# First feed-forward with four pairs by seven in seven of its groups, raw weight tiles also in unwritten places of its result, a fourth sum kept apart, another head and other ends

## Chip, core and metric

The kernel runs on one core of one Trainium2 chip. The metric is device time in microseconds (us) of one execution; the median of several runs is compared. A core has five engines that run their own instruction streams: PE (TensorE, matrix products; "PEld" are its weight loads), DVE (VectorE), ACT (ScalarE), POOL (GpSimd) and SP (SyncE, which here only issues DMAs). They wait for one another and for DMAs by semaphores.

## What is computed

One layer on x of 256 tokens by 2048, in float32, with 256 memory tokens. Cut to what matters here:

```python
def swiglu_ffn(h, w_in, w_out):
    gate, up = jnp.split(h @ w_in, 2, axis=-1)
    return (jax.nn.silu(gate) * up) @ w_out

x = x + 0.5 * swiglu_ffn(rms_norm(x, ffn1_norm), ffn1_w_in, ffn1_w_out)
...
x = x + memory_cross_attention(h, mem_n, w_q, w_kv, w_o)
x = x + 0.5 * swiglu_ffn(rms_norm(x, ffn2_norm), ffn2_w_in, ffn2_w_out)
return rms_norm(x, final_norm)
```

w_in is 2048 by 11264 (gate and up columns), w_out 5632 by 2048. The change touches h @ w_in of both feed-forwards (FF1, FF2), the start of the kernel, the end of the w_o product in front of FF2, and the final norm.

## The kernel before

**Split products.** A float32 operand a is held as hi = a rounded to fp32r and lo = a − hi. A product is hi·hi + hi·lo + lo·hi, so three matmuls. ACT makes hi by a cast, DVE lo by a subtraction (`parts`, L339 and L340); the pair of them is an `hl` tile.

**Groups.** A feed-forward's w_in product runs over 11 groups j of 512 gate and 512 up columns, and in a group over 16 row tiles k of 128 rows of w_in, taken in 8 pairs. A row tile of a group is a raw tile of 128x1024 (512 KB), loaded by SP (L349). Token columns are two halves of 128.
- A pair "by eight" (`eight`, through `by_two`: L288 x_hi·w_hi, L289 x_hi·w_lo, L291 x_lo·w_hi) is 2 row tiles with 12 matmuls of 512 columns each: 24.
- A pair "by seven" (`seven`, through `three`: L275, L276, L277) is Strassen's scheme in Winograd's form on a 2 by 2 block of row tiles and halves: seven products, 21 matmuls. It needs sums of raw tiles on DVE (L388, L389, L394, L401), which are split like weights, and sums of x (the "forms", made by `sides`, L368 to L376: two operations of ACT, four of DVE, a split).

A pattern of letters says which pair goes how: both feed-forwards have "SCSCSCCC" (S by seven, C by eight) in groups 1 to 10, 183 matmuls each; group 0 is plain, by eight throughout, 192. The results of the products 1 to 7 and of the eighth accumulator stay in eight PSUM banks through a group; behind the last S, ACT and DVE add them up (L439 to L443, L452), and `give` (L418, L420) makes silu(gate)·up into h[j].

**Accumulated weights.** For the row tiles in `SUMMED` (2, 7, 13 of each group but the first) the low part is made by a DMA: `summed` has ACT write −raw, rounded, into the low part (L358) and raw, rounded, into the high part (L359), and POOL issue a DMA that adds the weight onto the low part, so that raw − hi stands there (L360). It costs ACT one more pass and DVE none. FF1 has two such tiles (`hl_s`, and one in `more`, which takes x's place after group 0), FF2 one.

**Places.** Raw tiles cycle over four tiles of a pool and five places in `spare`; hl tiles over three of a pool, two in `ring`, in FF1 two more in `more`. In FF2, `spare` lies in the place that the attention's o_hl has before (tag S2), `ring` in S0.

**Head.** For k = 0 to 15 of FF1's group 0: SP loads two tiles of x (`x_arrives`), ACT and DVE make gain·x as hi and lo (`gained`, L239, L240), the weight is loaded, split and multiplied; `x_more` loads x once more by rows in four chunks of 512 KB at k = 5, 7, 9, 11, into raw tiles, and ACT squares them (L525) for the norm; at k = 6, 9, 12 the forms are made.

**Order.** A tile scheduler sets the order of each engine from the program's order and its own estimates; `issue_after` ties an instruction behind another. Engines take their instructions in order: a waiting one holds up all behind it. Per group SP issues 16 loads, ACT's and POOL's accumulations lie between the casts.

## Time and profile before

| | before |
|---|---|
| median of 3 runs | 2108.14 us (2107.7 to 2108.7) |
| profiled execution: its time | 2108.84 us |
| profiled execution: span from the first to the last instruction | 2107.0 us |
| PE busy | 2084.5 us (99%) |
| DVE busy | 1576.8 us (75%) |
| ACT busy | 1161.6 us (55%) |
| mean granted TensorE clock | 0.998 |

Rows of the timeline read: start, duration (both us), engine, line of the kernel, operation, output<-inputs, shape, count, and in brackets how long the engine had been idle before it and what released it. Matmuls overlap: a row's duration is longer than the distance to the next start. Rows of the waits read: what waited, for what, us in total, times, longest. Times in texts below are us from the span's start.

### The profile page before, as it was taken

To read this page: it belongs to the slowest core of one execution; us is meant where nothing else is said; L and a number is where in the kernel's file an instruction comes from. 1 tells how busy PE (TensorE), PEld (TensorE's weight loads), DVE (VectorE), ACT (ScalarE), POOL (GpSimd) and SP (SyncE) were. 2 spreads that over 40 slices of the span, in tenths; PEclk is the share of its full clock that TensorE was granted. 3 is DMA by queue.
4 is the path that set the end of the run, shared out by engine and by line. 5 is a ranking of instruction groups with operands and counts; after the bars stand their busy time and mean duration, and the time that the engine had idled before them with its cause. 6 is when DMAs were issued, how large, how long until landed. Compare 5 with 4: busy or idle time off the path is not lost.

```text
span 2107.0 us, 26590 instructions
## 1 busy us (share of the span) xinstructions
PE 2084.5 (99%) x9764; PEld 1738.5 (83%) x9764; DVE 1576.8 (75%) x2215; ACT 1161.6 (55%) x1450; POOL 67.7 (3%) x83
## 2 busy tenths in 40 slices
...
GB/s 360 230 227 257 229 238 245 263 167 169 216 198 188 206 236 200 190 176 185 176 201 185 186 154 111 206 281 191 231 259 247 232 229 250 178 160 202 197 192 149
DMA packets 122244, 442.34 MB, mean 210 GB/s; under 512 B 13697, under 2 KB 13825, under 8 KB 121729
## 3 DMA queue, kind: packets, MB, share of 16 engines
...
q10 hardware_dynamic: 288, 0.79, 0.1%
q14 instruction: 56, 0.45, 0.1%
...
## 4 chain that ended last, share of the span: by engine, by line
PE 84%; issue 11%; DMA 2%; ACT 1%; POOL 1%; DVE 1%; SPq 0%; POOLq 0%; ACTq 0%
PE acc L172 12%; PE acc L173 12%; PE acc L171 12%; PE acc L125 9%; PE acc L289 7%; PE acc L288 7%; PE acc L291 7%; PE acc L126 4%; PE acc L277 2%; PE acc L276 2%; PE acc L275 2%; PE aux L263 1%; PE acc L1066 1%; PE acc L1065 1%; PE acc L1067 1%
## 5 line engine op out<-in xcount | busy, mean ns | idle before, releaser
L113 DVE TENSOR_TENSOR hl<-raw,hl 128x1024 fp32r<-128x1024 f32 (+1 forms) x402 | 488.6, 1216 | 282.5 <-ACT hl L112 281.1
L112 ACT CAST hl<-raw 128x1024 fp32r<-128x1024 f32 (+1 forms) x402 | 419.7, 1045 | 481.6 <-PE acc L173 289.3
L339 ACT CAST hl<-spare 128x1024 fp32r<-128x1024 f32 (+1 forms) x135 | 131.8, 993 | 95.5 <-DVE spare L389 38.5
L340 DVE TENSOR_TENSOR hl<-spare,hl 128x1024 fp32r<-128x1024 f32 (+1 forms) x135 | 154.4, 1150 | 35.8 <-ACT hl L339 34.2
L288 PE MATMUL acc<-hl,x_hl 128*128 128x512 f32 x408 | 144.2, 394 | 9.7 <-ACT hl L339 9.7
L289 PE MATMUL acc<-hl,x_hl 128*128 128x512 f32 x408 | 149.9, 395 | 0.0
L340 DVE TENSOR_TENSOR hl<-raw,hl 128x1024 fp32r<-128x1024 f32 (+1 forms) x101 | 113.9, 1131 | 45.9 <-ACT hl L339 44.3
L339 ACT CAST ring<-spare 128x1024 fp32r<-128x1024 f32 (+1 forms) x99 | 97.2, 988 | 68.9 <-DVE spare L389 26.9
L340 DVE TENSOR_TENSOR ring<-spare,ring 128x1024 fp32r<-128x1024 f32 (+1 forms) x99 | 112.9, 1145 | 19.9 <-ACT ring L339 18.8
L291 PE MATMUL acc<-hl,x_hl 128*128 128x512 f32 x408 | 127.5, 392 | 0.0
L339 ACT CAST hl<-raw 128x1024 fp32r<-128x1024 f32 (+1 forms) x101 | 97.7, 977 | 51.8 <-PE acc L291 16.1
L172 PE MATMUL acc<-hl,x_hl 128*128 128x512 f32 x256 | 100.5, 392 | 0.2 <-DVE hl L113 0.2
L172 PE MATMUL acc<-hl,m_hl 128*128 128x512 f32 x256 | 100.4, 392 | 0.0
L173 PE MATMUL acc<-hl,m_hl 128*128 128x512 f32 x256 | 100.2, 391 | 0.0
L173 PE MATMUL acc<-hl,x_hl 128*128 128x512 f32 x256 | 99.8, 390 | 0.0
L288 PEld LDWEIGHTS acc<-hl,x_hl 128*128 128x128 f32 x408 | 76.8, 189 | 25.9 <-ACT hl L339 10.1
L289 PE MATMUL acc<-ring,x_hl 128*128 128x512 f32 x248 | 93.1, 389 | 0.0
L288 PE MATMUL acc<-ring,x_hl 128*128 128x512 f32 x248 | 91.2, 390 | 0.0
L171 PE MATMUL acc<-hl,m_hl 128*128 128x512 f32 x256 | 91.2, 393 | 0.0
L289 PEld LDWEIGHTS acc<-hl,x_hl 128*128 128x128 f32 x408 | 77.2, 190 | 16.9 <-DVE hl L340 1.1
L291 PEld LDWEIGHTS acc<-hl,x_hl 128*128 128x128 f32 x408 | 77.5, 190 | 16.4
L125 PE MATMUL acc<-x_hl,hl 128*128 128x512 f32 x256 | 91.0, 398 | 0.0
(359 smaller groups left out, 5173.9 us busy)
## 6 DMA issues: line engine op xcount, KB each, us to landing
spare<-in_ffn_w_in SPq DMA_DIRECT2D x192, 512.0 KB, 6.4
raw<-in_ffn_w_out SPq DMA_DIRECT2D x176, 512.0 KB, 3.8
raw<-in_ffn_w_in SPq DMA_DIRECT2D x160, 512.0 KB, 6.3
hl_s<-in_ffn_w_in POOLq DMA_DIRECT2D x44, 512.0 KB, 7.3
raw<-in_w_mix_vg SPq DMA_DIRECT2D x32, 512.0 KB, 4.6
raw<-in_w_k SPq DMA_DIRECT2D x32, 512.0 KB, 4.0
raw<-in_w_v SPq DMA_DIRECT2D x32, 512.0 KB, 4.4
raw<-in_w_mix_out SPq DMA_DIRECT2D x32, 512.0 KB, 4.6
```

Source lines behind the costliest of these rows:

```text
L112: nc.scalar.copy(out=hl[:, 0, :size], in_=raw[:, :size])
L113: newest[0] = nc.vector.tensor_tensor(out=hl[:, 1, :size], in0=raw[:, :size], in1=hl[:, 0, :size].bitcast(F32), op=ALU.subtract)
L125: nc.tensor.matmul(acc, lhsT=w_hi, rhs=x_hl, start=first, stop=False, skip_group_check=True)
L126: nc.tensor.matmul(acc[:, 0], lhsT=w_lo, rhs=x_hl[:, 0], start=False, stop=last, skip_group_check=True)
L171: nc.tensor.matmul(acc[t], lhsT=x[:, 0, s], rhs=hi[:, k], start=k0 + k == 0, stop=False)
L172: nc.tensor.matmul(acc[t], lhsT=x[:, 0, s], rhs=lo[:, k], start=False, stop=False)
L173: nc.tensor.matmul(acc[t], lhsT=x[:, 1, s], rhs=hi[:, k], start=False, stop=k0 + k == nk - 1)
L288: nc.tensor.matmul(acc[t][g], lhsT=x[:, 0, s], rhs=hi[:, cols[g]], start=(t, g) in first, stop=False)
L289: nc.tensor.matmul(acc[t][g], lhsT=x[:, 0, s], rhs=lo[:, cols[g]], start=False, stop=False)
L291: nc.tensor.matmul(acc[t][g], lhsT=x[:, 1, s], rhs=hi[:, cols[g]], start=False, stop=last)
L339: nc.scalar.copy(out=hl[:, 0, :n], in_=raw[:, :n])
L340: newest[0] = nc.vector.tensor_tensor(out=hl[:, 1, :n], in0=raw[:, :n], in1=hl[:, 0, :n].bitcast(F32), op=ALU.subtract)
```

## The change

- FF1: groups 1 to 7 go by "SCSCSCSC" (four pairs by seven), with the row tiles 2, 6, 7, 11 and 14 accumulated; groups 8 to 10 as before. Its raw tiles also cycle over h[j] tiles that aren't written yet (`h[max(j + 2, 7):]`); accumulated weights have raw places of their own, and `summed` for the next one is issued one row tile later.
- `seven`: the sum for product 4 is written into the free half of `sums`, ahead of the splits, no longer into `two`.
- FF2: group 0 goes by "SCSCSCCC" too, 183 matmuls instead of 192. Its forms are made beside the w_o product, behind x's tiles 1, 5 and 9, with a raw tile as scratch; `ring` is allocated there.
- Head: 11 matmuls of 128 columns on a tile of ones, whose result isn't used; x's first tile and FF1's gains come in one DMA on ACT's queue; the first weight in two halves, each split by itself; x's chunks for the squares at k = 2, 4, 6, 8 into h[7] to h[4]; forms at k = 6, 9, 12, 15.
- End: three of the four sums of squares are added up ahead of the last; the last enters the root and the mean directly; a tensor_scalar takes the place of a scalar_tensor_tensor.

By count of the order, 8460 matmuls of 512 columns become 8430; those of 256 columns stay 964; those of 128 columns become 304 + 11.

```diff
-PATTERNS = ("SCSCSCCC", "SCSCSCCC")
-SUMMED = ((2, 7, 13), (2, 7, 13))
+FOUR, THREE = "SCSCSCSC", "SCSCSCCC"
+SUMMED = {FOUR: (2, 6, 7, 11, 14), THREE: (2, 7, 13)}
+WARM = 11
...
+    gx = xt.tile([P, 2 * KD + KD * T], F32, name="gx", tag="x")
+    gains, xT = gx[:, KD:2 * KD], gx[:, 2 * KD:].rearrange("p (k t) -> p k t", t=T)
+    nc.scalar.dma_start(out=gx[:, KD:2 * KD + T], in_=a["gains_x0"])
+    nc.scalar.dma_start(out=xT[:, 1], in_=a["xT"][:, 1])
+    nc.vector.memset(ones, 1.0)
+    idle = pa.tile([P, 2, T], F32, name="aux")
+    for _ in range(WARM):
+        nc.tensor.matmul(idle[:, 0, :P], lhsT=ones, rhs=ones, start=True, stop=True)
+    nc.scalar.activation(out=st.tile([P, 1], F32, name="warm"), in_=ones[:, 0:1], func=AF.Silu)
...
+    def sides(k, gain, form, xg, f):
+        xg = xg.rearrange("p (k t) -> p k t", k=2)
+        f = f.rearrange("p (f n) -> p f n", f=4)
+        for q in range(2):
+            nc.scalar.activation(out=xg[:, q], in_=xT[:, k + q], func=AF.Copy, scale=gain(k + q))
+        a11, a21, a12, a22 = xg[:, 0, :P], xg[:, 0, P:], xg[:, 1, :P], xg[:, 1, P:]
+        nc.vector.scalar_tensor_tensor(out=f[:, 0], in0=a21, scalar=-1.0, in1=a22, op0=ALU.mult, op1=ALU.subtract)
+        nc.vector.scalar_tensor_tensor(out=f[:, 1], in0=f[:, 0], scalar=-1.0, in1=a11, op0=ALU.mult, op1=ALU.subtract)
+        nc.vector.tensor_tensor(out=f[:, 2], in0=a11, in1=a21, op=ALU.subtract)
+        nc.vector.tensor_tensor(out=f[:, 3], in0=a12, in1=f[:, 1], op=ALU.subtract)
+        split(form[:, :, 0], form[:, :, 1], f)
...
+            self.raws_summed = [self.raws.pop()]
...
+            raws = self.raws + [h.rearrange("p a b -> p (a b)") for h in self.h[max(j + 2, NG - 4):]]
+            i = self.raw_at % (4 + len(raws))
             self.raw_at += 1
-            raw = wraw.tile([P, 1024], F32, name="raw") if i < 4 else self.raws[i - 4]
+            raw = wraw.tile([P, 1024], F32, name="raw") if i < 4 else raws[i - 4]
             nc.sync.dma_start(out=raw, in_=self.w_in[j, :, k])
...
-            raw, hl = self.raw(j, k), self.hls[at % len(self.hls)]
+            raw, hl = self.raws_summed[at % len(self.hls)], self.hls[at % len(self.hls)]
+            nc.sync.dma_start(out=raw, in_=self.w_in[j, :, k])
...
+            nc.vector.tensor_tensor(out=sums[:, lo], in0=two[:, lo], in1=one[:, lo], op=ALU.subtract)
...
-            nc.vector.tensor_tensor(out=two[:, lo], in0=two[:, lo], in1=one[:, lo], op=ALU.subtract)
-            w = self.parts(two, G)
+            w = self.parts(sums, G)
             three(b["4"], self.x(k + 1, 1), w[:, 0, lo], w[:, 1, lo], first, False)
+            if self.next is not None:
+                with tc.issue_after(self.cast.ins):
+                    self.summed(self.next)
+                self.next = None
...
-                if at is not False:
-                    self.summed(at + len(self.hls))
+                if self.next is not None:
+                    with tc.issue_after(self.cast.ins):
+                        self.summed(self.next)
+                self.next = None if at is False else at + len(self.hls)
...
+        def rooted(self, root):
+            r = root()
+            nc.scalar.activation(out=st.tile([P, 1], F32, name="warm"), in_=ones[:, 0:1], func=AF.Silu)
+            self.summed(0)
+            return r
+        def early(self, before):
+            self.raw_at += 1
+            self.at += 1
+            raw = wraw.tile([P, 1024], F32, name="raw")
+            hl = whl.tile([P, 2, 1024], F32R, name="hl")
+            halves = [slice(G, 2 * G), slice(0, G)]
+            for s in halves:
+                nc.sync.dma_start(out=raw[:, s], in_=self.w_in[0, :, 0, s])
+            x = before(0)
+            for s in halves:
+                with tc.issue_after(x.ins):
+                    split(hl[:, 0, s], hl[:, 1, s], raw[:, s])
+            return hl
+        def run(self, root, before=None, after=None, more=None, early=False):
+            self.sums_at = [(j, k) for j in range(1, NG) for k in SUMMED[self.patterns[j]] if j < NG - 1 or k < 13]
+            if early:
+                acc = token_accs()
+                for k in range(KD):
+                    if k == 0:
+                        w = self.early(before)
+                    else:
+                        before(k)
+                        w = self.parts(self.raw(0, k))
+                    begin = [(t, g) for t in range(2) for g in range(2)] if k == 0 else []
+                    by_two(acc, self.x_hl[:, k], w[:, 0], w[:, 1], k, begin, k == KD - 1)
+                    after(k)
+                    if k == 13:
+                        r = self.rooted(root)
+                self.give(0, [acc[t][0] for t in range(2)], [acc[t][1] for t in range(2)], r)
+                if more is not None:
+                    more()
+                    self.summed(1)
+            else:
+                r = self.group(0, None, root=root)
...
-        raw = wraw.tile([P, 1024], F32, name="raw")
+        raw = ff.h[7 - c].rearrange("p a b -> p (a b)")
...
-            if k in (5, 7, 9, 11):
-                x_squares(k // 2 - 2)
-            if k in (6, 9, 12):
+                nc.sync.dma_start(out=pv, in_=a["pv"])
+            if k in (2, 4, 6, 8):
+                x_squares(k // 2 - 1)
+            if k in (6, 9, 12, 15):
...
-        ff = FeedForward(stack, ("S1", "S0", "S2"), x_hl, "ffn1_norm", a["ffn1_w_in"], PATTERNS[0], SUMMED[0])
+        ff = FeedForward(stack, ("S1", "S0", "S2"), x_hl, lambda k: gains[:, k:k + 1], a["ffn1_w_in"], [FOUR] * 8 + [THREE] * (NG - 8))
...
+            ring = big.tile([P, 4, 2, 1024], F32R, name="ring", tag="S0")
+            done = [2 * p + 1 for p, c in enumerate(THREE) if c == "S"]
...
+                if f in done:
+                    raw = wraw.tile([P, 1024], F32, name="raw")
+                    sides(f - 1, lambda k: col("ffn2_norm", k), forms_in(ring)[done.index(f)], raw[:, :512], raw[:, 512:])
...
-        ff = FeedForward(stack, ("S0", "S1", "S2"), x_hl, "ffn2_norm", a["ffn2_w_in"], PATTERNS[1], SUMMED[1])
+        ff = FeedForward(stack, ("S0", "S1", "S2"), x_hl, lambda k: col("ffn2_norm", k), a["ffn2_w_in"], [THREE] * NG, ring)
...
-            tot, v, s, r = [st.tile([P, 1], F32, name=f"{n}{t}") for n in ("f_tot", "f_v", "f_s", "f_r")]
-            nc.vector.reduce_sum(out=tot, in_=sums[:, t], axis=AX.X)
-            nc.scalar.activation(out=s, in_=tot, func=AF.Sqrt, scale=1.0 / D, bias=eps)
-            nc.vector.tensor_scalar(out=v, in0=tot, scalar1=1.0 / D, scalar2=RMS_EPS, op0=ALU.mult, op1=ALU.add)
+            v, s, r = [st.tile([P, 1], F32, name=f"{n}{t}") for n in ("f_v", "f_s", "f_r")]
+            last = sums[:, t, 3:4]
+            nc.scalar.activation(out=s, in_=last, func=AF.Sqrt, scale=1.0 / D, bias=most[t])
+            nc.vector.tensor_scalar(out=v, in0=last, scalar1=1.0 / D, scalar2=most[t], op0=ALU.mult, op1=ALU.add)
             nc.vector.reciprocal(out=r, in_=s)
-            nc.vector.scalar_tensor_tensor(out=r, in0=v, scalar=r, in1=s, op0=ALU.mult, op1=ALU.add)
+            nc.vector.tensor_scalar(out=r, in0=v, scalar1=r, scalar2=s, op0=ALU.mult, op1=ALU.add)
...
+        most = [st.tile([P, 1], F32, name=f"f_most{t}") for t in range(2)]
+        for t in range(2):
+            nc.vector.reduce_sum(out=most[t], in_=sums[:, t, 0:3], axis=AX.X)
+            nc.vector.tensor_scalar(
+                out=most[t], in0=most[t], scalar1=1.0 / D, scalar2=RMS_EPS, op0=ALU.mult, op1=ALU.add
+            )
```

At the start of the program, PE's first rows were those of row tile 0 (`acc` the accumulators, `hl` the split weight, `x_hl` the split x):

```order
L288 MATMUL acc<-hl,x_hl 128x512 x4
L289 MATMUL acc<-hl,x_hl 128x512 x2
L291 MATMUL acc<-hl,x_hl 128x512 x2
L289 MATMUL acc<-hl,x_hl 128x512 x2
L291 MATMUL acc<-hl,x_hl 128x512 x2
L288 MATMUL acc<-hl,x_hl 128x512 x4
```

and are now

```order
L203 MATMUL aux<-ones 128x128 x11
L302 MATMUL acc<-hl,x_hl 128x512
L303 MATMUL acc<-hl,x_hl 128x512
L305 MATMUL acc<-hl,x_hl 128x512
L302 MATMUL acc<-hl,x_hl 128x512 x2
L303 MATMUL acc<-hl,x_hl 128x512
L302 MATMUL acc<-hl,x_hl 128x512
L305 MATMUL acc<-hl,x_hl 128x512
L303 MATMUL acc<-hl,x_hl 128x512
L305 MATMUL acc<-hl,x_hl 128x512
```

The 11 idle matmuls stand first; then the first row tile begins with one accumulator, whose three products come together, since the weight comes by halves.

In FF1's groups ACT makes the accumulated tiles between the casts (`hl_s` and `more` the two tiles that are accumulated onto, `raw` and `spare` raw weights; the brackets name the semaphores waited for, DMASW that of an accumulating DMA). Before, at the turn from group 1 to group 2:

```order
L339 CAST ring_117<-spare_118 128x1024 [waits PE_49,Activation_49]
L339 CAST more_475<-raw_859 128x1024 [waits DMAHW4_49,PE_49,Activation_49]
L418 ACTIVATE h1_107<-spare_118,r_x2_95 128x512 [waits DVE_49]
L339 CAST hl_882<-raw_861 128x1024 [waits DMAHW5_49,PE_49,Activation_49]
L358 ACTIVATE more_475<-raw_838 128x1024 [waits DMAHW0_49,DMASW3_49,PE_49]
L359 CAST more_475<-raw_838 128x1024 [waits PE_49]
L339 CAST hl_892<-raw_861 128x512 [waits DVE_49,Activation_49]
L339 CAST hl_899<-spare_118 128x1024 [waits DMAHW0_49,Activation_49]
L339 CAST ring_117<-spare_118 128x1024 [waits PE_49,Activation_49]
```

Now, in group 5, for its row tiles 11 and 14 (on the tiles that row tiles 6 and 7 leave):

```order
L378 CAST ring_131<-raw_1885 128x1024 [waits DMAHW6_49,PE_49,Activation_49]
L378 CAST hl_1875<-spare_132 128x512 [waits DVE_49]
L399 ACTIVATE more_498<-spare_132 128x1024 [waits DMAHW7_49,DMASW5_49,PE_49]
L400 CAST more_498<-spare_132 128x1024 [waits PE_49]
L399 ACTIVATE hl_s_133<-spare_132 128x1024 [waits DMAHW2_49,DMASW6_49,PE_49]
L378 CAST ring_131<-spare_132 128x1024 [waits DVE_49,Activation_49]
L400 CAST hl_s_133<-spare_132 128x1024 [waits PE_49,Activation_49]
L378 CAST more_498<-raw_1913 128x1024 [waits DVE_49,DMAHW1_49,PE_49,Activation_49]
L378 CAST hl_1937<-raw_1915 128x1024 [waits PE_49,Activation_49]
```

Two accumulations (L399, L400) now stand next to one another, where one stood alone; each waits for the low matmuls that read its tile last, and the casts behind wait with it. On PE there are, in the order, 54, 41, 41, 57, 41, 38 and 34 matmuls of 512 columns between the last low matmul on the tile that row tile 7 uses and the first low matmul of row tile 7, in groups 1 to 7; 48 to 50 for row tile 11; more than 53 for the others. Before, the smallest such distance was 103 in FF1 and 43 in FF2.

At the start of FF2, PE went from w_o's last matmuls (L126) on to plain products of group 0:

```order
L126 MATMUL acc_11040<-o_hl_9109,hl_11064 128x256
L125 MATMUL acc_11040<-o_hl_9109,hl_11064 128x512
L126 MATMUL acc_11040<-o_hl_9109,hl_11064 128x256
L288 MATMUL acc_11114<-hl_11120,x_hl_10402 128x512 [waits Activation_49]
L288 MATMUL acc_11115<-hl_11120,x_hl_10402 128x512 [waits PE_49]
```

and now goes to products of the first pair by seven:

```order
L128 MATMUL acc_11116<-o_hl_9157,hl_11140 128x512
L129 MATMUL acc_11116<-o_hl_9157,hl_11140 128x256
L128 MATMUL acc_11116<-o_hl_9157,hl_11140 128x512
L129 MATMUL acc_11116<-o_hl_9157,hl_11140 128x256
L289 MATMUL acc_11189<-hl_11203,ring_10452 128x512 [waits Activation_49]
L289 MATMUL aux_11190<-hl_11203,ring_10452 128x512
L290 MATMUL acc_11189<-hl_11203,ring_10452 128x512 [waits DVE_49]
```

On DVE, at the same place, `xT` is the residual's last tile, and `spare` the place of the sums. Now:

```order
L379 TENSOR_TENSOR ring_10452<-raw_11237,ring_10452 128x1024 [waits DMAHW4_49,Activation_49]
L253 SCALAR_TENSOR_TENSOR x_hl_10450<-xT_3513,pv_82,x_hl_10450 128x256 [waits Activation_49]
L229 TENSOR_TENSOR ss_10451<-ss_10451,sq_11113 128x256 [waits Activation_49]
L265 SCALAR_TENSOR_TENSOR xT_3513<-acc_11116,xT_3513 128x256 [waits PE_49]
L416 TENSOR_TENSOR spare_11187<-raw_11197 128x512 [waits DMAHW2_49]
L417 TENSOR_TENSOR spare_11187<-raw_11199,raw_11197 128x512 [waits DMAHW3_49]
L265 SCALAR_TENSOR_TENSOR xT_3513<-acc_11116,xT_3513 128x256 [waits DVE_49]
L422 TENSOR_TENSOR raw_11197<-spare_11187,raw_11199 128x512 [waits DVE_49]
L379 TENSOR_TENSOR hl_11203<-spare_11187,hl_11203 128x1024 [waits Activation_49]
```

The weight that PE needs first (hl_11203) is the split of a sum in `spare`; the sums stand behind the residual of w_o's last product (acc_11116), half of which lies between them. Before, the weight needed first was split straight from a raw tile.

112 lines of the change are left out of this document (42 added, 70 removed).

## The prediction

> **What bounds the kernel now.** I read the page's busy shares and its chain first, then TensorE's (PE's) waits, then windows by stage. All times are us.
>
> ```profile
> PE 2084.5 (99%) x9764; PEld 1738.5 (83%) x9764; DVE 1576.8 (75%) x2215; ACT 1161.6 (55%) x1450; POOL 67.7 (3%) x83
> PE 84%; issue 11%; DMA 2%; ACT 1%; POOL 1%; DVE 1%; SPq 0%; POOLq 0%; ACTq 0%
> ```
> ```profile
> PE acc L288 <- ACT hl L339: 9.7, 2, 7.1
> PE acc L289 <- DMA hl_s<-in_ffn_w_in: 1.0, 2, 0.7
> PE acc L275 <- ACT h L418: 0.5, 1, 0.5
> ```
> ```profile
> 10.00:60.00 50.00, 46.95 (x195) 37.44 (x194) 33.32 (x54) 37.22 (x54) 1.88 (x2) 0.97 0.91 340
> 160.00:210.00 50.00, 50.00 (x223) 41.40 (x222) 40.30 (x49) 32.18 (x36) 3.48 (x4) 1.00 0.79 251
> 1320.00:1380.00 60.00, 60.00 (x348) 52.49 (x347) 45.54 (x72) 32.01 (x46) 0.00 (x0) 1.00 0.62 199
> ```
>
> PE is busy 99% and carries the chain. It waits about 12 us in the whole program, 9.7 of them at two places of the head. So two things pay: fewer matmuls, and the head. The windows (columns: PE, weight loads, DVE, ACT, POOL, granted clock, DMA share, GB/s) show the head below clock 1.00 and with PE gaps of 3 in 50; in the feed-forward's steady stage (160 to 210) PE has no gap, DVE is at 81%, ACT 64%, the DMA engines 79%.
>
> **1. Fewer matmuls.** One matmul of 512 columns in the steady stream costs its start-to-start distance:
>
> ```profile
> 17.39 0.39 PE L288 MATMUL acc<-ring,x_hl 128*128 128x512 f32 x1
> ...
> 22.84 0.39 PE L288 MATMUL acc<-hl,x_hl 128*128 128x512 f32 x1
> ```
> Between these rows lie two row tiles k of 12 matmuls: 5.45/24 = 0.227 each, 2.72 per k. A pair by eight has 24, by seven 21. In the order, FF1 has one pair more by seven in groups 1 to 7 (21 matmuls fewer), FF2 three in group 0 (9 fewer): **−4.8 and −2.0**.
>
> **2. Head.**
> ```profile
> 6.01 1.04 ACT L339 CAST hl<-raw 128x1024 fp32r<-128x1024 f32 x1 [0.47 <-DMA raw<-in_ffn_w_in]
> ```
> ```profile
> 7.11 2.07 PE L288 MATMUL acc<-hl,x_hl 128*128 128x512 f32 x4 [7.11 <-ACT hl L339]
> 11.96 1.07 PE L288 MATMUL acc<-hl,x_hl 128*128 128x512 f32 x4
> ...
> 41.63 0.61 PE L291 MATMUL acc<-hl,x_hl 128*128 128x512 f32 x2
> 44.82 1.50 PE L288 MATMUL acc<-hl,x_hl 128*128 128x512 f32 x4 [2.58 <-ACT hl L339]
> ...
> 49.34 0.39 PE L288 MATMUL acc<-ring,x_hl 128*128 128x512 f32 x1
> ...
> 57.53 0.39 PE L275 MATMUL acc<-ring 128*128 128x512 f32 x1
> ```
> ```profile
> L239 ACT ACTIVATE x_hl<-xT,pv 128x256 fp32r<-128x256 f32 x16 | 7.1, 500 | 1.6 <-DMA pv<-in_pv 1.1 <-DMA xT<-in_xT 0.4
> ```
> ```profile
> 42.69 1.06 ACT L525 ACTIVATE raw<-raw 128x1024 f32<-128x1024 f32 x1 [1.92 <-DMA raw<-in_x]
> 43.74 1.03 ACT L339 CAST hl<-raw 128x1024 fp32r<-128x1024 f32 x1
> ```
> Group 0 runs from 7.11 to 57.53, 50.4, where 192 matmuls need 43.6. Lost are 4.85 − 2.72 = 2.1 in its first k (half clock after the start), and at 41.6 to 49.3 the wait of 2.58 plus 4.52 − 2.72 = 1.8 at half clock behind it. The wait comes from ACT: the square of an x chunk waits for its load, and the cast that PE needs is queued behind it.
>
> After, the first weight comes as two halves of 256 KB, x's first tile and the gains on ACT's queue, and 11 idle matmuls run from about 1. I estimate PE's first product at 5.5 (the 6.01 cast of 1.04 replaced by a half one about 0.4 earlier and 0.5 shorter, and less queued ahead) at full clock. The transfers and ACT then bound it: at 340 GB/s (91% DMA share) a weight of 512 KB takes 1.5 and x's tile of 128 KB 0.4, an x chunk of 512 KB every second k 0.8 more per k, 2.7 in all; on ACT a k costs 1.04 for the cast, 0.5 for the gained x, and half a square (0.5) and a third of the sides, some 2.5. Both are as slow as PE's 2.72, so what PE gains at its start (1.6 + 2.1 = 3.7) can't grow, and some of it is lost while it catches up with the loads: I take 3 of it. The x chunks are now loaded into places of h that nobody holds, three k earlier, so the wait at 42 and its slow clock (2.58 + 1.8 = 4.4) should go; late next is the weight itself, which by then has a lead. Sum **−7.3** (3.0 + 4.4, less 0.1 for the new order). Ends: −8.3 if loads keep pace from the start, −2.9 if the chunk's wait only moves.
>
> The Trainium skill, "TensorE: Matmul & The Clock Gate", Part 1, says that the array starts at half clock, goes to full after about 3.4 us of sustained work, and falls back after an idle window of about 3.4 us. The start agrees (4.4 us of slow matmuls); the wait of 2.58 had half clock behind it already, so here a shorter gap was enough.
>
> **3. FF1's accumulations.** Five weights per group instead of three get their low part from an accumulating DMA. A tile's cycle:
>
> ```profile
> 1728.37 0.39 PE L289 MATMUL acc<-hl_s,x_hl 128*128 128x512 f32 x1
> ...
> 1738.11 0.39 PE L288 MATMUL acc<-hl_s,x_hl 128*128 128x512 f32 x1
> 1739.22 0.50 PE L289 MATMUL acc<-hl_s,x_hl 128*128 128x512 f32 x1 [0.72 <-DMA hl_s<-in_ffn_w_in]
> ```
> ```profile
> 1728.79 1.06 ACT L358 ACTIVATE hl_s<-spare 128x1024 fp32r<-128x1024 f32 x1 [1.17 <-PE acc L289]
> ```
> ```profile
> 1730.26 0.89 POOL L360 DMA_DIRECT2D hl_s<-in_ffn_w_in  x1 [12.06 <-ACT hl_s L358]
> ```
> ```profile
> hl_s<-in_ffn_w_in POOLq DMA_DIRECT2D x1, 512.0 KB, 8.9
> ```
> ```profile
> DMA to landing us min/median/max: 5.3/7.3/9.8
> ```
> From the last low matmul on the tile (1728.37) to the next one possible: 0.42 to ACT, 1.47 to the issue, the landing L, 0.06: **1.95 + L**. L is 8.9 here (the row of DMA issues, in us to landing), and PE waits 0.7: FF2 has one tile, whose distance is 43 matmuls, 9.75. FF1 has two tiles, so its distances were above 23; with five per group the one at k=7 shrinks, counted in the order of groups 1 to 7, to 54, 41, 41, 57, 41, 38, 34 matmuls: 12.2, 9.3, 9.3, 12.9, 9.3, 8.6, 7.7. At k=11 it is 48 to 50, about 11. All others exceed 12.
>
> ```profile
> q1 hardware_dynamic: 2304, 8.39, 53.4%
> q0 software_dynamic: 432, 1.57, 21.2%
> ```
> These are 42 us of group 2 (packets, MB, share): weights take 22.4, three accumulations 8.9. Five take 14.8; with 37.2 of a group of 40.8 the DMA engines are 91% full, against 75%. What L is within 5.3 to 9.8 hangs on the raw loads beside it:
>
> ```profile
> 178.55 0.86 POOL L360 DMA_DIRECT2D hl_s<-in_ffn_w_in  x1 [14.78 <-ACT hl_s L358]
> ```
> ```profile
> 179.75 0.85 SPq L349 DMA_DIRECT2D raw<-in_ffn_w_in  x2
> 181.13 2.43 SPq L349 DMA_DIRECT2D spare<-in_ffn_w_in  x2
> ```
> This one found no load in flight and got the first rivals 1.2 later: it landed in 5.3, the least. At k=7 PE is deep in a pair by seven, whose raw tiles come free late, and SP has in the order one load to issue beside it; so I take L = 6 there (a wait of 0.25 in group 7 alone) and 8.5 at k=11 (none). With 0.7 for one or two late ones as in FF2, **+1**; ends 0 and +6.4 (first rival). A wait here blocks PE's later matmuls, and through PE the casts.
>
> The Trainium skill, "DMA: Bandwidth & Descriptors", Queues, rings and completion order, says each DMA engine round-robins between queues packet by packet. By that rule an accumulation shares with the loads but isn't queued behind a backlog, so L stays near the shared values, and the sum near +1 to +6; the spread of 5.3 to 9.8 agrees.
>
> **4. DVE and ACT in FF1.**
> ```profile
> 112.37 1.22 DVE L340 TENSOR_TENSOR ring<-spare,ring 128x1024 fp32r<-128x1024 f32 x1
> ```
> ```profile
> 94.62 0.68 DVE L389 TENSOR_TENSOR spare<-raw 128x512 f32<-128x512 f32 x1
> ```
> A pair by seven has 4 sums (0.68) and 3.5 splits (1.22): 7.0. It replaces 2 splits (2.4), and two more accumulations save 2 more: +2.2 per group. DVE's 81% of 41.5 is 33.4; 35.6 of 40.8 is 87%, ACT near 67%. Raw tiles gain h's unwritten places, so the loads have more lead. The fourth sum, now kept beside, frees product 4 of waiting for products 2 and 3. PE's waits list of before has no wait on a low part of L340, so I cost the 2.2 at **0**; ends −1 (the freed product) and +2 (what the 87% would leave open in one group).
>
> **5. Start of FF2.**
> ```profile
> 1386.34 0.28 PE L126 MATMUL acc<-o_hl,hl 128*128 128x256 f32 x1
> 1386.46 0.62 PE L288 MATMUL acc<-hl,x_hl 128*128 128x512 f32 x2
> ```
> ```profile
> 1388.50 0.88 DVE L251 SCALAR_TENSOR_TENSOR xT<-acc,xT 128x256 f32<-128x256 f32 x2
> ```
> Before, plain products follow w_o's last matmul without a gap. After, group 0 opens with a pair by seven whose weight sums are written into `spare`, which takes o_hl's place: they can begin only when w_o's last matmul is done. DVE's order then is half a residual (0.42), two sums (0.60 from start to start each, the last 0.68), ACT's cast (1.04), with 0.06 at each of four handovers and 0.28 for the last matmul: PE has nothing for **3.1**. As the 2.58 before had 1.8 of half clock behind it, I add 1.9: **+5.0**. Ends 3.1 and 6.5 (the second pair's loads also go into spare, only after it is free). The forms for x are made beside w_o, where DVE has 24% free (45.54 of 60) and ACT 47%: 0, and up to 1 without that cover.
>
> **6. End.**
> ```profile
> 2099.40 0.16 DVE L1025 TENSOR_REDUCE f_tot<-sums 128x1 f32<-128x4 f32 x1 [0.79 <-ACT sq L1019]
> 2099.59 0.15 DVE L1027 TENSOR_SCALAR f_v<-f_tot 128x1 f32<-128x1 f32 x1
> ...
> 2100.11 0.60 DVE L1029 SCALAR_TENSOR_TENSOR f_r<-f_v,f_r,f_s 128x1 f32<-128x1 f32 x1
> ```
> The reduction leaves the chain (2099.40 to 2099.59), and L1029 becomes an operation like L1027's: −0.2 − 0.45 = **−0.65**.
>
> **Sum:** −4.8 − 2.0 − 7.3 + 1 + 0 + 5.0 − 0.65 = −8.75. The profiled run took 2108.84 (span 2107.0), 0.7 above the median of 2108.14; so 2100.1 by its own measure, **2099.4** as a median.
>
> **Rivals.**
> - *Accumulations land late* (L = 8.2 throughout, chain 10.15): the five short distances cost 0.85 three times, 1.5 and 2.4, 6.4 in all: 2104.8. For it speak 16 points more of DMA load, against it the one load beside k=7.
> - *The fuller queue turns the kernel slower.* If L is 10 everywhere, the chain is 11.95: 2.65 three times, 3.3 and 4.2 at k=7, about 0.8 six times at k=11: 20 instead of 1, 2118. It decides from L = 9.5 on (14.6 of waits, 2113). Against it: 9.8 is the largest seen.
> - *The head keeps its chunk wait*: −2.9 instead of −7.3, 2103.8. For it: DMA at 91%; against: the chunks start three k earlier.
> - *FF2 starts at full clock*: +3.1, 2097.5.
> - *The change removes nothing*: excluded, the order has 30 matmuls of 512 columns fewer.
>
> **How the numbers follow.** A measurement of this kernel tells about 0.2% (4.2 us) from no change, so faster is below 2103.9, slower above 2112.4. Chances: forecast 0.64 (2096 to 2103), late accumulations 0.14, head 0.10, FF2 at full clock 0.06, slower 0.06. Faster: forecast, FF2, and 0.08 of late accumulations and head (their near ends), 0.78; same 0.16; slower 0.06. Low end: all good ends of terms 2, 3 and 5, −12.7, 2095.4. The high end takes in the late accumulations with an FF2 start of +6.5: 2106.
>
> **What would show it.** Group 0 ends near 50, and PE waits there for no cast longer than 1; PE's waits for accumulations are about 1 in all, at k=7; one gap of 3 at FF2's start with slow matmuls behind; steady groups of 40.8. Wrong if the accumulating DMA's waits exceed 6, or if DVE's 87% shows as PE waits on low parts inside the groups by FOUR.

## The result and the profile after

The kernel became slower: median 2137.51 us (2133.53 to 2138.86, 4 runs) against 2108.42 of the kernel before on the same chip, ratio **1.0132** [1.0117, 1.0147]. The profiled execution took 2136.83, its span is 2134.9. Of the runs below, one of e8 took 5659.87 us and one of e12 2301.46; medians and ratios are given without these two.

The page of the kernel after, busy shares and chain:

```profile
PE 2101.3 (98%) x9756; PEld 1740.3 (82%) x9756; DVE 1605.3 (75%) x2276; ACT 1192.5 (56%) x1489; POOL 80.0 (4%) x97
PE 69%; issue 24%; DMA 3%; POOL 2%; ACT 1%; DVE 1%; SPq 0%; POOLq 0%; DVEq 0%; ACTq 0%
```
PE has fewer matmuls to do and is busy 17 us longer: up to its last matmul it has 20.5 us of half clock instead of 3.4, and some matmuls became slower at full clock too. PE's waits after, and three windows (columns as before):

```profile
PE acc L303 <- DMA hl_s<-in_ffn_w_in: 7.5, 8, 2.3
PE acc L128 <- ACT hl L115: 4.0, 1, 4.0
PE acc L289 <- DVE spare L489: 3.1, 1, 3.1
PE acc L289 <- ACT hl L378: 2.9, 1, 2.9
PE acc L302 <- ACT ring L378: 1.8, 1, 1.8
PE acc L303 <- DMA more<-in_ffn_w_in: 1.1, 2, 0.9
```
```profile
10.00:60.00 50.00, 48.20 (x205) 38.93 (x204) 38.34 (x63) 39.84 (x58) 1.88 (x2) 0.97 1.03 391
160.00:210.00 50.00, 49.39 (x217) 40.36 (x217) 45.25 (x56) 33.78 (x38) 4.43 (x6) 1.00 0.92 268
1320.00:1380.00 60.00, 55.98 (x309) 48.66 (x308) 46.56 (x82) 33.95 (x54) 0.00 (x0) 0.94 0.68 225
```
The start's wait of 7.1 is out of the list because the idle matmuls now run in it; the first product stands at 5.77 instead of 7.11. The head's second wait, 2.58 at 44.8 before, is 1.80 at 30.2 now. New are one in the w_o stage (4.0, with the clock at 0.94 in its window), one in group 6 of FF1 (3.1) and the one at FF2's start (2.9). The waits for accumulations went from two with 1.0 us to ten with 8.6. The DMA share in FF1's groups rose from 0.79 to 0.92.

The starts of PE's first and last matmuls of each stage, read from the traces, give where the 27.8 us of span came from. The last column is the run e17 below, with the causes taken out.

| stage, us | before | after | difference | e17 |
|---|---|---|---|---|
| to the first product | 7.11 | 5.77 | −1.3 | 6.23 |
| FF1 group 0 (192 matmuls) | 50.42 | 48.00 | −2.4 | 44.07 |
| FF1 groups 1 to 10 | 417.53 | 426.03 | **+8.5** | 413.27 |
| up to w_o | 810.83 | 812.78 | +2.0 | 812.50 |
| w_o | 100.45 | 106.90 | **+6.4** | 100.17 |
| gap to FF2 | 0.12 | 3.15 | +3.0 | 0.12 |
| FF2 w_in, 11 groups | 461.52 | 472.71 | **+11.2** | 459.76 |
| FF2 w_out | 248.66 | 249.75 | +1.1 | 248.66 |
| end | 10.40 | 9.78 | −0.6 | 9.25 |

**Head.** ACT's and PE's timeline of the kernel after:

```profile
27.07 0.61 ACT L123 CAST ring<-spare 128x512 fp32r<-128x512 f32 x1
27.70 1.28 ACT L217 ACT_TABLE_LOAD   x1
29.00 0.20 ACT L217 ACTIVATE rt<-rv 128x2 f32<-128x2 f32 x1
29.11 1.03 ACT L378 CAST ring<-h 128x1024 fp32r<-128x1024 f32 x1
```
```profile
27.78 0.61 PE L305 MATMUL acc<-hl,x_hl 128*128 128x512 f32 x2
30.19 1.09 PE L302 MATMUL acc<-ring,x_hl 128*128 128x512 f32 x3 [1.80 <-ACT ring L378]
```
A cast for PE stands behind the root and its table load: it begins at 29.11, while its weight, by the trace, had landed at 27.30. The root follows the last square of a chunk, which ended at 43.7 before and ends at 25.1 now; so its 1.3 us on ACT fall into the time when loads are late (DMA share 1.03 in the window). The granted clock is half from 30.9 to 34.3.

**FF1, group 6.** PE and DVE:

```profile
263.77 0.40 PE L291 MATMUL aux<-ring 128*128 128x512 f32 x1
267.27 0.79 PE L289 MATMUL acc<-ring,x_hl 128*128 128x512 f32 x1 [3.10 <-DVE spare L489]
```
```profile
252.72 0.69 DVE L417 TENSOR_TENSOR spare<-raw 128x512 f32<-128x512 f32 x1 [5.91 <-DMA raw<-in_ffn_w_in]
...
261.86 0.69 DVE L417 TENSOR_TENSOR spare<-spare 128x512 f32<-128x512 f32 x1 [0.89 <-DMA spare<-in_ffn_w_in]
```
DVE waited for raw loads, 5.91 and then 0.89, and what it does for PE came late in a row. The load behind the long wait was issued at 240.19 and landed at 252.63; accumulations issued at 239.21 and 243.13 were under way beside it, and the DMA share between 240 and 255 was 0.94. The matmul behind the wait takes 0.79 where others take 0.39, which is half clock (266.4 to 273.2). The Trainium skill, "TensorE: Matmul & The Clock Gate", Part 1, speaks of a free-running idle window of about 3.4 us. Half clock followed waits of 3.1 and of 1.8 here, so in this case shorter ones were enough. Length alone doesn't decide it: PE waited 2.28 for an accumulation up to 1707.8, and no half clock followed.

**w_o.** SP's waits and timeline, and ACT's timeline:

```profile
SPq L389 <- PE acc L136: 16.5, 1, 16.5
```
```profile
1316.70 1.75 SPq L389 DMA_DIRECT2D h<-in_ffn_w_in  x4
1318.56 14.87 SPq L112 DMA_DIRECT2D raw<-in_w_o  x7
```
```profile
1325.61 0.62 ACT L115 CAST hl<-raw 128x512 fp32r<-128x512 f32 x1 [0.89 <-DMA raw<-in_w_o]
```
SP takes its DMAs in order. Four loads of FF2's weights into h tiles stand ahead of w_o's loads. Their place is held by the attention until 1316.7; w_o's weights wait behind them.

**FF2's start.** PE's timeline:

```profile
1399.48 0.28 PE L129 MATMUL acc<-o_hl,hl 128*128 128x256 f32 x1
1402.63 0.50 PE L289 MATMUL acc<-hl,ring 128*128 128x512 f32 x1 [2.87 <-ACT hl L378]
```
The distance is 3.15. In the trace DVE and ACT do in it what the prediction counted: half a residual, two sums, the cast.

### The profile page after: what moved, and what is told of

It is laid out like the page before. It is cut to its first block, busy times and chain, and to the rows that moved or that the text cites. A ratio compares the mean times of both kernels' runs of the same rounds, so it can differ in the third digit from the quotient of the medians.

```text
span 2134.9 us, 26710 instructions
## 1 busy us (share of the span) xinstructions
PE 2101.3 (98%) x9756; PEld 1740.3 (82%) x9756; DVE 1605.3 (75%) x2276; ACT 1192.5 (56%) x1489; POOL 80.0 (4%) x97
## 4 chain that ended last, share of the span: by engine, by line
PE 69%; issue 24%; DMA 3%; POOL 2%; ACT 1%; DVE 1%; SPq 0%; POOLq 0%; DVEq 0%; ACTq 0%
PE acc L175 12%; PE acc L176 12%; PE acc L174 12%; PE acc L128 8%; PE acc L129 4%; PE acc L303 4%; PE acc L302 3%; PE acc L305 3%; POOL hl_s L401 1%; PE aux L277 1%; PE acc L290 1%; PE acc L291 1%; PE acc L289 1%; DMA hl_s<-in_ffn_w_in 1%; PE acc L1134 1%
## 5 line engine op out<-in xcount | busy, mean ns | idle before, releaser
L116 DVE TENSOR_TENSOR hl<-raw,hl 128x1024 fp32r<-128x1024 f32 (+1 forms) x402 | 488.2, 1215 | 281.8 <-ACT hl L115 280.9
L115 ACT CAST hl<-raw 128x1024 fp32r<-128x1024 f32 (+1 forms) x402 | 419.4, 1045 | 476.8 <-PE acc L176 294.7
L379 DVE TENSOR_TENSOR ring<-spare,ring 128x1024 fp32r<-128x1024 f32 (+1 forms) x85 | 88.8, 1050 | 35.8 <-ACT ring L378 34.0
L378 ACT CAST ring<-spare 128x1024 fp32r<-128x1024 f32 (+1 forms) x85 | 76.7, 912 | 63.4 <-PE acc L305 27.4
L379 DVE TENSOR_TENSOR hl<-raw,hl 128x1024 fp32r<-128x1024 f32 x69 | 83.9, 1219 | 19.2 <-ACT hl L378 19.2
L128 PE MATMUL acc<-o_hl,hl 128*128 128x512 f32 x256 | 91.5, 400 | 4.0 <-ACT hl L115 4.0
L128 PE MATMUL acc<-x_hl,hl 128*128 128x512 f32 x256 | 91.0, 398 | 0.0
L128 PE MATMUL acc<-y_hl,hl 128*128 128x512 f32 x256 | 90.5, 399 | 0.0
L401 POOL DMA_DIRECT2D hl_s<-in_ffn_w_in x51 | 44.6, 875 | 1208.2 <-ACT hl_s L399 617.5
L378 ACT CAST hl<-raw 128x1024 fp32r<-128x1024 f32 x69 | 71.8, 1051 | 30.6 <-PE acc L305 16.1
L175 PE MATMUL acc<-hl,hA 128*128 128x512 f32 x224 | 87.1, 392 | 0.0
```

Of the source, the lines that this page charges most:

```text
L115: nc.scalar.copy(out=hl[:, 0, :size], in_=raw[:, :size])
L116: newest[0] = nc.vector.tensor_tensor(out=hl[:, 1, :size], in0=raw[:, :size], in1=hl[:, 0, :size].bitcast(F32), op=ALU.subtract)
L128: nc.tensor.matmul(acc, lhsT=w_hi, rhs=x_hl, start=first, stop=False, skip_group_check=True)
L175: nc.tensor.matmul(acc[t], lhsT=x[:, 0, s], rhs=lo[:, k], start=False, stop=False)
L378: self.cast = nc.scalar.copy(out=hl[:, 0, :n], in_=raw[:, :n])
L379: newest[0] = nc.vector.tensor_tensor(out=hl[:, 1, :n], in0=raw[:, :n], in1=hl[:, 0, :n].bitcast(F32), op=ALU.subtract)
```

## Experiments

Ratios are to the kernel before on the same chip; the kernel after is 1.0132. "Waits" of a stage are the sums of PE's gaps over 0.1 us outside half clock: in FF1's groups 0.9 before and 8.7 after, in FF2's 1.6 and 9.4.

### What stands in SP's queue ahead of w_o (e1, e6, e10)

e1 keeps h out of the raw places of FF2's group 0, e6 out of all of FF2; e10 is e6 with tiles of their own for the forms' scratch, which is a raw tile of the pool of four. `early_x` is true in FF1.
```diff
-            raws = self.raws + [h.rearrange("p a b -> p (a b)") for h in self.h[max(j + 2, NG - 4):]]
+            raws = self.raws + [h.rearrange("p a b -> p (a b)") for h in self.h[max(j + 2, NG - 4):] if j or self.early_x]  # e1
+            raws = self.raws + [h.rearrange("p a b -> p (a b)") for h in self.h[max(j + 2, NG - 4):] if self.early_x]  # e6, e10
...
-                    raw = wraw.tile([P, 1024], F32, name="raw")
+                    x = [ev.tile([P, T], F32, name="tu") for _ in range(2)]
+                    f01, f23 = [ev.tile([P, T], F32, name="tg") for _ in range(2)]
```


> The changed kernel, but FF2's group 0 takes no raw tiles in h. Theory (queue): four loads of FF2's weights into h stand in SP's queue ahead of w_o's loads and wait 16.5 us for places that the attention holds, so w_o's weights come late: without them the wait of 4.0 us at 1322 and the half clock behind it go, 6 us faster than the changed kernel (2131.5 against 2137.5), and the loads of w_o are issued without a gap. Rival (sides): the forms that are made beside w_o block ACT and DVE there: the wait stays, within 1 us of the changed kernel.

> The changed kernel, but FF2 takes no raw tiles in h at all. Theory (queue): no load of FF2 stands ahead of w_o's loads in SP's queue any more; the wait of 3.4 to 4.2 us at 1322 and the half clock behind it go, 5.5 us, and w_o takes 100.5 us as before instead of 106 to 107. Theory (run-ahead): with 8 places instead of 12 the raw loads run less far ahead and leave the accumulating DMAs more of the engines: FF2's waits for them (7.5 us) fall to 1 to 3. Together 9 to 12 us faster than the changed kernel. Rival (sides): w_o stays at 106. Rival (order of the accumulations, issued one row tile later): FF2's waits stay at 7 to 8.

> The kernel without h in FF2 (e6), and the forms that are made beside w_o have their scratch in small tiles of their own, not in a raw tile of the pool of four. Theory (two blocks in SP's queue): in e6 a load of w_o waited 9.7 us for the forms' scratch; with both blocks gone w_o takes 100.5 to 101.5 us as before and no wait for a cast over 1 us is left there: 5 us faster than e6. Rival (the forms' work on ACT and DVE stands ahead of the casts): w_o stays at 105 or more.

Measured: e1 2131.8, 1.0111 [1.0094, 1.0129], w_o 105.9; e6 2130.86, 1.0106 [1.0089, 1.0123], w_o 106.8; e10 2125.92, 1.0094 [1.0079, 1.0110], w_o **101.5**. SP's timeline of e1, SP's waits of e6 and PE's waits of e10 between 1290 and 1400 show why:

```profile
1313.26 1.75 SPq L390 DMA_DIRECT2D h<-in_ffn_w_in  x4
```
```profile
SPq L112 <- DVE raw L334: 9.7, 1, 9.7
```
```profile
PE acc L289 <- ACT hl L379: 2.9, 1, 2.9
PE acc L134 <- ACT p_hl L123: 0.6, 1, 0.6
```
In e1 the four loads, now those of group 1, still stood there: the edit missed. In e6 they are gone and w_o's load waits 9.7 for the forms' scratch instead. Only without both does PE's wait at L128 vanish. These are two blocks in one queue. The scratch is enough by itself (e6); whether the loads into h are, no run shows. The forms' own work costs next to nothing: e11 below makes none beside w_o and takes 101.5 there as well. e6's second theory, fewer loads ahead in FF2, was worth little: FF2's groups took 470.3 instead of 472.7.

### Places, and the fifth accumulated tile (e2, e7)

From group 6 on, the cycle of places loses one h per group, so that the position in it jumps: by a count of the program's order, a place is used again after 6 to 8 loads at the start of group 6, after 16 in groups 4 and 5. e2 takes the least recently used free place; e7 leaves out the accumulation of k = 7.
```diff
-            i = self.raw_at % (4 + len(raws))
+            place = next(p for p in self.places if p[0] == "w" or p in free)    # e2
+            self.places.remove(place)
+            self.places.append(place)
...
-SUMMED = {FOUR: (2, 6, 7, 11, 14), THREE: (2, 7, 13)}
+SUMMED = {FOUR: (2, 6, 11, 14), THREE: (2, 7, 13)}                          # e7
```


> The changed kernel, but each raw load takes the place that was used longest ago, in place of a count modulo a number of places that shrinks by one per group from group 6 on. Theory (jump): where the modulus changes, the count jumps to places used 5 to 7 loads earlier instead of 15, loads wait for them, and PE waits at 263 (5 to 6 us with the half clock) and at 1705 (2.5 to 3): both go, 6 to 9 us faster than the changed kernel. Rival (more accumulations alone fill the DMA queue and make all of these waits): both stay, within 1.5 us of the changed kernel.

> The changed kernel, but groups 1 to 7 of FF1 accumulate four weights (2, 6, 11, 14) instead of five; row tile 7 is split by DVE. Theory (short distance): FF1's waits for accumulating DMAs (3.6 us) come from row tile 7, whose distance is 34 to 41 matmuls: they go to under 1. The stall at 263 stays, since it comes from the places of the raw loads. Rival (all of FF1's loss is DMA load): with 4 instead of 5 the stall at 263 goes too, 6 us more. Rival (DVE is the bound): one more split per group makes FF1 slower by 1 to 4 us.

Measured: e2 2126.8, 1.0094 [1.0079, 1.0109], FF1's groups 421.2, the stall at 263 gone; FF2's no shorter (474.7). e7 2124.04, 1.0073 [1.0054, 1.0091], FF1's groups **415.4**. PE's waits in FF1's groups, all of them, in e7:

```profile
PE aux L289 <- DVE spare L479: 0.5, 2, 0.2
```
e7 was expected to keep the stall, and it is gone. With four accumulations the count still jumps in group 6 (places used again after 4 to 6 loads), so the stall needs both, the jump and the fifth transfer: either edit ends it. The fifth tile costs FF1 10.6 in this kernel.

### Where tiles lie (e3, e5)

x's tile now also holds the gains: 128 bytes more per partition, and what is allocated behind it (hl_s, h, the w_out product's hC) moves by that, against ring, x_hl and the hl tiles, which don't. Matmuls with such an operand became slower. e3 moves all tiles by 64 bytes; e5 gives the gains a tile of their own.
```diff
+    const.tile([P, 16], F32, name="to_64")                                  # e3
...
-    gx = xt.tile([P, 2 * KD + KD * T], F32, name="gx", tag="x")
+    gains = const.tile([P, KD], F32, name="gains")                          # e5
+    xT = xt.tile([P, KD, T], F32, name="xT", tag="x")
```


> The changed kernel, but all tiles lie 64 bytes further on, by an unused tile of 64 bytes (before, tiles began 64 bytes past a multiple of 128; after, on a multiple). Theory (address): the matmuls that read hl_s, hC and held take 0.233 instead of 0.227 us for where these lie: their distance goes back to 0.227, 4 to 7 us faster than the changed kernel. Rival (something else in the change, or the execution): the distances stay at 0.232 for hl_s, time within 1.5 us.

> The changed kernel, but the gains lie in a tile of their own and x's tile has its old size of 16384 bytes, so that every large tile begins where it began before the change. Theory (relative place): in the changed kernel hl_s, h, hC and held lie 128 bytes off the others' grid of 8192 bytes (x's tile with the gains has 16512 bytes), and matmuls whose weights and moving data lie on different grids take 0.233 instead of 0.227 us; an offset of all tiles by 64 bytes changed nothing. Back on one grid, hl_s's rows have 0.227 again and the excess of 2.7 us in FF1, 3.0 in FF2 and 1.7 in the stages between goes: 6 to 8 us faster than the changed kernel. Rival (accumulating DMAs or the order slow these matmuls): the excess stays, within 1.5 us.

Measured: e3 2134.36, 1.0130 [1.0111, 1.0150]; e5 2125.18, **1.0077** [1.0062, 1.0092]. FF2's matmuls on hl_s (ns min/median/max) before, after, in e3 and in e5:

```profile
L288 PE MATMUL acc<-hl_s,x_hl x112: 387/389/402, 1448.4 to 1825.5; 128*128 128x512 f32 x112
```
```profile
L302 PE MATMUL acc<-hl_s,x_hl x108: 388/397/404, 1450.1 to 1824.5; 128*128 128x512 f32 x108
```
```profile
L303 PE MATMUL acc<-hl_s,x_hl x109: 388/397/398, 1445.0 to 1828.1; 128*128 128x512 f32 x109
```
```profile
L303 PE MATMUL acc<-hl_s,x_hl x112: 387/389/395, 1441.8 to 1827.2; 128*128 128x512 f32 x112
```
The distance from start to start rose from 0.227 to 0.232 or 0.233 for these. Summed over the matmuls of 512 columns, what lies above 0.2268 (gaps aside) is 0.2 + 0.2 + 10.5 before in FF1's groups, FF2's and the stages between, 2.7 + 3.0 + 12.1 after, and 0.7 + 0.7 + 10.5 in e5: 7 us lost, 6 got back. FF2's w_out product, which isn't in these sums, has 2.3, 4.1 and 2.2: 1.8 more lost and got back. Most of the rest of e5's gain is its head (44.1).

### The head (e4)

```diff
-        raw = ff.h[7 - c].rearrange("p a b -> p (a b)")
+        raw = ff.h[6 - c].rearrange("p a b -> p (a b)")
...
-            if k in (2, 4, 6, 8):
+            if k in (5, 7, 9, 11):
```


> The changed kernel, but x's chunks for the squares are loaded and squared at k = 5, 7, 9, 11 as before the change, into h[6] to h[3]. Theory (head): the chunks, the root and its table load were moved into the stretch in which the transfers are full, and ACT's queue held the casts up behind them: the wait of 1.8 at 28 and its half clock go, 3 to 4 us faster than the changed kernel. Rival: the chunk's wait comes back at 42 as before the change, within 1 us of the changed kernel or slower.

Measured: 2134.24, 1.0133 [1.0115, 1.0150]; group 0 took 44.17, 3.8 less, but FF1's groups 427.2 and the time stayed. One profile can't carry this: over all profiles with the chunks early (11, all but one of them with other edits) group 0 took 43.7 to 48.0, median 46.3; over the eight with the chunks at their old places (e4, e12 to e18) 43.9 to 44.7, median 44.1. So, as far as runs with other edits can tell, early chunks cost about 2 and don't always.

### FF2's start, and the raw tile of an accumulation (e8, e11, e9)

e8 has FF2's group 0 plain again; e11 also makes the forms in FF2 as before, without h. e9 takes the summed raw tile from the cycle again.
```diff
-            if early:
+            if before is not None:                                          # e8, e11
...
-        turns = ff.run(lambda: rms_cols(ss, D, "r_x2"))
+        turns = ff.run(lambda: rms_cols(ss, D, "r_x2"), lambda k: None, lambda k: None)
...
-            raw, hl = self.raws_summed[at % len(self.hls)], self.hls[at % len(self.hls)]
+            raw, hl = self.raw(j, k), self.hls[at % len(self.hls)]          # e9
```


> The changed kernel, but FF2's group 0 goes by eight again (192 matmuls); the forms are still made beside w_o. Theory (start): the gap of 3.1 us behind w_o and the half clock behind it (1.9) go, nine matmuls (2.0) come back: 2.5 to 3.5 us faster than the changed kernel, and the first matmul of FF2 follows w_o's last within 0.2 us. Rival: the stall of w_o's loads, which the loads into h cause here too, shifts the first casts and a gap of over 1 us stays.

> The kernel without h in FF2 (e6), and FF2's group 0 by eight with the forms beside it, as before the change: nothing is made beside w_o. w_o takes 100.5 us, FF2's first matmul follows at once, nine matmuls more: against e6 minus 6.3 (w_o), minus 3.1 (gap), minus 1.9 (half clock), plus 2.0: 9 us faster than e6, and FF2's waits for accumulating DMAs stay at 5 to 6. Rival (w_o is slow for another reason than the forms): w_o stays at 105.

> The changed kernel, but the weights that are accumulated onto take their raw tiles from the common cycle again, as before the change, not from places of their own. Theory (own place): the next such load waits in SP's queue until ACT has copied the one before (SP waits 116 us for that in the changed kernel), which is half a microsecond behind the accumulating DMA's issue: it and the loads held up behind it run beside every accumulation, which lands 0.7 to 1 us later than before. Taken from the cycle, that wait goes, FF2's waits for accumulating DMAs fall from 7 to 2 or less, FF1's by 1 to 2: 6 to 8 us faster than the changed kernel. Rival (only the amount of DMA work counts): FF2's waits stay at 6 to 8, within 1.5 us.

Measured: e8 2126.19, 1.0077 [1.0056, 1.0099], FF2 follows w_o after 0.12 again, its groups 475.2; e11 2121.38, 1.0071 [1.0057, 1.0085], w_o 101.5, groups 469.6; e9 2140.93, 1.0161 [1.0147, 1.0175], **slower** still, FF2 481.3 with waits of 15.4. e11 gains 9 against e6 as it was priced, w_o, start and nine matmuls together. But against the 461.5 before, FF2's groups stay 8 too long in e11, 14 in e8 and 20 in e9, and the summed raw's place isn't their cause.

### All of it together, and what was left in FF2 (e12 to e18)

e12, expected 9 to 11 us faster than the kernel before, joins six edits: places as in e2 without h in FF2, chunks as in e4, gains as in e5, four accumulations as in e7, FF2's start as in e11, the summed raw from the cycle as in e9. FF1's groups and w_o came out as expected, FF2's not. What then differed from before in FF2's code were two things: the accumulation is issued one tile later, and the fourth sum is written into `sums`, early in DVE's order, not over its raw tile behind two casts. T undoes the one, W the other.
```diff
-                self.next = None if at is False else at + len(self.hls)
+                if at is not False:                                         # T
+                    self.summed(at + len(self.hls))
...
-            nc.vector.tensor_tensor(out=sums[:, lo], in0=two[:, lo], in1=one[:, lo], op=ALU.subtract)
-            w = self.parts(sums, G)
+            nc.vector.tensor_tensor(out=two[:, lo], in0=two[:, lo], in1=one[:, lo], op=ALU.subtract)
+            w = self.parts(two, G)                                          # W
```


> All mends together: the place used longest ago, x's chunks later, gains in their own tile, no h in FF2, four accumulated weights in FF1's groups 1 to 7, raw tiles of accumulated weights from the cycle, FF2's start as before. What is left of the change: four pairs by seven in FF1's groups 1 to 7 (4.8 us), the head (6 us) and the end (0.6 us). If the parts add up: head 44.1, FF1 412 to 414 against 417.5, w_o 100.5, FF2 461.5 to 463 against 461.5: 9 to 11 us faster than the kernel before, ratio 0.995 to 0.996. Rival (the parts need one another's cover, DVE at 87% is the bound): FF1 stays at 416 or more, ratio 0.997 to 1.000.

> Five edits as in the run of all six, but the summed raw tiles keep places of their own. Theory, the late issue: the second feed-forward waits because its accumulations are issued one tile later than before; the place of their raw tile matters little, so its stage stays near 470 us and the run near 2105 (ratio 0.997 to 1.000). Rival, the place: with the places of the cycle the summed raw alone cost 3.6 us as the single edit, so here the stage is 3 to 6 us shorter than 469.6 and the run 2099 to 2102.

> The run before with the accumulation of the next summed tile issued behind the sixteen matmuls of the last one, as before the change, and not one tile later. Late issue: an accumulation gets back some 5 to 7 us of lead, the waits for hl_s in the second feed-forward fall from about 7 to under 2 us, its stage comes to 462 to 465 us and the run to 2094 to 2100 (ratio 0.993 to 0.997). Rival, the fourth sum's place in VectorE's order: nothing moves, the stage stays at 467 to 470 us. A third: issued at once, the casts of the summed tile stand ahead of the next tile's cast on ScalarE and the first feed-forward loses 1 to 3 us.

> Issued at once, and the summed raw tile from the cycle, which is how both feed-forwards issued it before the change. Late issue: as in the run before within 2 us, stage 462 to 465 us, run 2095 to 2100. Rival, the fourth sum's place: stage 467 to 470 us, run 2102 to 2105.

> As the run before, and the fourth sum of a pair by seven written over its raw tile and behind the forms' casts, as before the change: the second feed-forward's code is then that of the kernel before. Both theories: its stage within 1.5 us of the 461.5 before, run 2094 to 2098. What this run is worth over the run before is the fourth sum's own share: late issue says 0 to 1 us, its rival 5 to 8. If the stage stays above 466 us, the cause is not in the code of this stage but in where its tiles lie.

> All six edits and the fourth sum written over its raw tile again, but the accumulation still issued one tile later. In the traces, where an accumulation of the second feed-forward is read soonest (7.85 us behind its issue), VectorE's earlier fourth sum frees a raw tile earlier and SP has two more loads under way with it. If that is the cause alone, its stage is 460 to 462 us and the run 2095 to 2098; if the two edits share it, as the steps 469.6, 465.0, 460.3 us read, 464 to 466 us and the run 2099 to 2102; if late issue alone puts the loads there, 468 to 470 and 2103 to 2105.

> The fastest kernel so far (issued at once, fourth sum over its raw tile) with the change's five accumulated tiles in a group again instead of four. If the fifth (k = 7, one tile behind k = 6) is too much for its place whatever the order, the first feed-forward goes from 413.1 to 420 us or more and the run to 2102 or more, as four against five gave 10 us on the changed kernel. If it was the loads under way with it, the stage stays within 2 us of 413 and the run within 3 us of 2096.

| run | edits | median | ratio | FF1 groups | FF2 groups | FF2 waits |
|---|---|---|---|---|---|---|
| e12 | all six | 2104.63 | 0.9988 [0.9979, 0.9997] | 413.0 | 469.6 | 9.6 |
| e13 | e12, summed raw's own place | 2106.71 | 0.9999 [0.9989, 1.0008] | 414.4 | 469.8 | 9.7 |
| e14 | e13 and T | 2106.65 | 0.9995 [0.9986, 1.0005] | 416.0 | 468.1 | 8.1 |
| e15 | e12 and T | 2102.77 | 0.9975 [0.9963, 0.9987] | 413.6 | 465.0 | 4.9 |
| e16 | e12, T and W | 2095.72 | 0.9941 [0.9927, 0.9956] | 413.1 | 460.3 | 0.4 |
| e17 | e12 and W | **2095.43** | 0.9948 [0.9931, 0.9964] | 413.3 | **459.8** | 0.0 |
| e18 | e16, five accumulated | 2101.03 | 0.9975 [0.9964, 0.9986] | 417.6 | 462.4 | 2.5 |

My theory of the late issue fell. From e12 on, T takes off 4.6 in FF2 (from e13 on only 1.7), but W alone 9.9, and T on top of W nothing. Steps taken in one order (469.6, 465.0, 460.3) had read like two causes; e17 shows that the fourth sum is enough. In one stretch of FF2, SP, POOL, DVE and PE of e12, then SP, POOL and DVE of e17:

```profile
1578.58 2.08 SPq L393 DMA_DIRECT2D raw<-in_ffn_w_in  x2
1582.28 0.33 SPq L393 DMA_DIRECT2D spare<-in_ffn_w_in  x1
...
1581.72 0.88 POOL L404 DMA_DIRECT2D hl_s<-in_ffn_w_in  x1 [14.29 <-ACT hl_s L402]
...
1576.13 0.68 DVE L426 TENSOR_TENSOR spare<-raw 128x512 f32<-128x512 f32 x1
...
1590.18 0.50 PE L304 MATMUL acc<-hl_s,x_hl 128*128 128x512 f32 x1 [0.44 <-DMA hl_s<-in_ffn_w_in]
```
```profile
1582.88 0.33 SPq L393 DMA_DIRECT2D raw<-in_ffn_w_in  x1
1583.31 0.38 SPq L393 DMA_DIRECT2D spare<-in_ffn_w_in  x1
...
1582.06 0.88 POOL L404 DMA_DIRECT2D hl_s<-in_ffn_w_in  x1 [14.30 <-ACT hl_s L402]
...
1582.13 0.69 DVE L432 TENSOR_TENSOR raw<-raw 128x512 f32<-128x512 f32 x1
```
In e12 DVE takes the fourth sum (L426) off its raw tile early, the tile is free earlier, and SP has issued two weight loads of 512 KB in the 3.1 us before the accumulation. In e17 DVE writes that sum over the raw tile at 1582.13, the next load follows its end, and no load is issued in those 3 us; the two come 0.8 and 1.3 behind the accumulation. Over all 29 accumulations of FF2, SP issued in the 3.1 us ahead of one 1.34 loads on average in e12, 1.03 in the kernel after, 0.69 in e17 and in the kernel before. ACT's and POOL's part is the same in both: the transfer shares the DMA engines with more. Its landing (us min/median/max over FF2's groups) in e12, and in e17:

```profile
DMA to landing us min/median/max: 7.5/8.4/10.6
```
```profile
DMA to landing us min/median/max: 5.4/7.1/9.6
```
The Trainium skill, "DMA: Bandwidth & Descriptors", Queues, rings and completion order, has each DMA engine take turns between queues by packets; an accumulation slowed by the loads under way with it agrees with that.

e18 puts the fifth accumulation back on the order of e16: FF1's groups take 4.5 more. PE's first waits of e18 in FF1's groups:

```profile
PE acc L304 <- DMA more<-in_ffn_w_in: 2.1, 3, 1.1
PE acc L290 <- ACT ring L379: 1.0, 1, 1.0
```
So in that kernel the fifth tile costs less than half of e7's 10.6. The rest hung on the places, or on another of the edits that e18 has and e7 hasn't; no run separates them.

## Why the prediction was wrong

Forecast 2099.4 (2095.4 to 2106.0), measured 2137.5: the sign too. Point by point:

1. **Fewer matmuls, −4.8 and −2.0: right as a term, as far as measured.** e17, with the 21 matmuls fewer in FF1, has its groups 4.3 below before; FF2's −2.0 no run measured by itself. What was wrong is the price of a matmul: it was taken as 0.227 from the kernel before and assumed to hold. Where tiles were moved by the gains it did not (e5): **+7**, and 1.8 in FF2's w_out product, a term that was missing.
2. **Head, −7.3: mis-sized**, −3.8 by the end of group 0 (57.53 to 53.77). The rival "keeps its chunk wait" (−2.9) was nearer. The step that failed is that chunks loaded three k earlier take the wait away: the loads then coincide with the weights' (share 1.03) and the wait falls on a cast behind the root. With chunks at the old k, in h, and the rest of the new head, group 0 ends at 49.48 in e4 and at 50.30 in e17, −8 and −7.2, and the wait at 42 is gone too: that the sum of −7.3 is near these is no merit of the earlier loading. The idle matmuls did most of what was expected: by the traces full clock was granted from 6.98, 1.2 behind the first product, instead of 4.3 behind it (11.43) before, so that three matmuls were slow instead of ten.
3. **FF1's accumulations, +1: the largest miss.** FF1's groups took 8.5 more where 4.8 less was due, 13.3 in all; 2.5 of it is the slower matmuls, 10.8 waits and half clock. The landing was counted with one load beside k = 7; nearness to raw loads was argued from the order and not followed through the places, whose cycle jumps (e2). L, taken as 6 at k = 7 and 8.5 at k = 11, was, by the order of the issues, 7.2 and 9.1 in the median of groups 1 to 7. The rival of late accumulations named the right resource, but only 2.8 of PE's waits there are for an accumulation. The stall of 3.1 in group 6, with some 3 us lost to the half clock behind it (half of the 6 from 267.3 to 273.2), came from raw loads that were late for DVE; the rest are small waits. Over the whole kernel the waits for accumulations are 8.6, mostly in FF2 (5.8), beyond the 6 that the prediction itself had named as the sign of being wrong.
4. **DVE and ACT, 0.** DVE's share was no bound, as said. But "the fourth sum, now kept beside, frees product 4" was weighed for FF1 alone, and for what it frees on PE. `seven` serves FF2 as well, and what it freed was a raw tile: about **10** in FF2 (e12 against e17). FF2's steady groups had no term in the sum at all.
5. **FF2's start, +5.0: right.** The gap is 3.15 (3.1 said) and half clock stands behind it from 1403.0 to 1406.4; e8 and e11 take it away. The bound on the forms ("0, and up to 1") held for their work on DVE and ACT (e10), but not for what they bring: SP's queue ahead of w_o was not looked at, and the loads into h and the scratch tile hold it up, **+6.4**.
6. **End, −0.65: right in kind**, −0.62 in the span's last stage, but that stage takes 9.15 to 10.1 over the runs that have the same end. On DVE, from the first operation behind the last sum to the last scaling, it is 1.55 before (2099.40 to 2100.95) and 1.03 after (2127.25 to 2128.28): −0.5.

The terms for FF2's start and the end held. The missing ones (7 for slower matmuls, 6.4 in w_o, 10 of waits and half clock in FF1 beyond the 1, 8 in FF2, 3.5 of the head) come to 35 of the 38 between forecast and result; between the two profiled spans it is 36.6, and FF2's w_out product has 1.1 of what is left. The slower rival, accumulations at L = 10 everywhere, was not what happened: the landing's median in FF2 rose from 7.3 to 8.7, in FF1 from 8.2 to 8.4.

Open: why FF2 loses 2 when FF1 has five accumulations (e18), and the 1 to 2 us of the stages between in nearly all runs. The loads into h in FF2 without the scratch in a raw tile were not tried, so the share of each block in w_o stays open.
